# Down projections in rows, in groups of 1024 columns, with seven block products for eight in a third of the k-tile pairs, and weights in 8 KB pieces

## The chip, the cores and the metric

The kernel runs on one core of a Trainium2 chip. A core has a matrix engine (TensorE, PE in the profile), a vector engine (VectorE, DVE), a scalar engine (ScalarE, ACT), a general one (GpSimd, POOL) and a sequencer that issues the DMA transfers here (SyncE, SP). They run side by side, each in the order of its own queue, and wait for one another by semaphores. The metric is the device time of one execution in microseconds; lower is better.

## The reference

Two layers act on a residual stream x of 256 tokens by 2048 features, all in float32. Cut to what matters:

```
for l in range(2):
    h = rms_norm(x, attn_norm[l])
    # w_in: 2048 x 6728; three kinds of heads, 16 in all, and a lightning index
    mixed = concat(moba(h @ w_in), diff(h @ w_in), dsa(h @ w_in))
    x = x + mixed @ w_out[l]                        # 2048 x 2048
    h = rms_norm(x, cross_norm[l])
    x = x + cross_attention(h, mem) @ cross_wo[l]   # 4 heads, 256 memory tokens
    h = rms_norm(x, ffn_norm[l])
    u = h @ ffn_w_up[l]                             # 2048 x 11008
    uc = causal convolution of u over 3 tokens, plus bias
    g, val = split(uc)                              # 5504 features each
    x = x + (silu(g) * val) @ ffn_w_down[l]         # 5504 x 2048
```

The last line of the loop is what the change rewrites: 256 tokens, 5504 inner features (43 k-tiles of 128), 2048 columns.

## The kernel before

TensorE multiplies rounded numbers, so each factor is split in two: a rounded part ("hi") and the rest ("lo", raw minus hi). A product is acts_hi · W_hi + acts_lo · W_hi + acts_hi · W_lo, the product of the two rests being left out. For the weights `load_split` does this: SP issues the load of a piece into the buffer `raw` (L181), ACT rounds it into `hi` (L184) and DVE subtracts, raw − hi, into `lo` (L186). A piece is 4 KB on each partition (2 k-tiles by 512 columns or 4 by 256); there are five buffers for raw and four each for hi and lo. Acts are split by `split`: L163 on ACT, L169 on DVE.

Two helpers hold the matmuls. `mm_rows` has tokens on the output's partitions: for each k-tile and each of two token tiles three matmuls 512 columns wide (L207, L208, L209). `up_acc` has features on the output's partitions: for each k-tile and each of two feature tiles one matmul 512 wide (L231, the weights' rounded part against the 256 hi and 256 lo acts side by side) and one 256 wide (L232, the weights' rest).

The residual stream lives transposed, features on partitions, in `xT`. `residual` adds a projection to it: for each of 8 pairs of feature tiles it runs `up_acc`, copies the second half out of PSUM (L284, ACT), adds (L287, L288, DVE), multiplies by the next norm's gain and splits (L163, L169) and sums squares (L296 on ACT, L297 on POOL).

The down projection of layer 0 is such a `residual` call: 8 pairs of outputs, 43 k-tiles each. That of layer 1 goes by rows: four calls of `mm_rows` on 512 columns, whose results are added (L941) to the stream's rows, which 32 transposes on TensorE (L930) have brought back meanwhile, and stored (L942). The acts of the down projection are split once, in `gate`, at the end of the up stage. That stage is `up_acc` with a convolution behind it (L887 to L895).

The order of the work comes from a tile framework: pools hand out buffers by tag, a piece's write waits until the buffer's last reader is done, and every engine's queue follows the order in which the program was written, moved a little by the framework. `kp` is a pool of 53 slots of 2 KB a partition, for rows, transposed acts and heads. Attention, norms and transposes stand in generators ("flows"); `tick` (L141), called after each weight piece, lets those that are due take a step.

Of the kernel before, what the change touches and what calls it, by code (L numbers as in the profile page):

```python
# [32 lines left out]
FIRST_COL = 3328  # L33

# [6 lines left out]
def hybrid_trunk(ctx: ExitStack, tc: tile.TileContext, x, mem, positions, attn_norm, w_in,  # L41
# [7 lines left out]
    kp = ctx.enter_context(tc.tile_pool(name="kp", bufs=53))  # L49
# [5 lines left out]
    def slot(dt=F32):  # L55
        return kp.tile([P, CH], dt, tag="k", name="k")
# [10 lines left out]
    # ---------------------------------------------------------------- residual stream and constants  # L67
# [6 lines left out]
    for c in range(NCH):  # L74
        xrow.append([slot() for _ in range(NT)])
        for t in range(NT):
            nc.sync.dma_start(xrow[c][t], x[0, t * P:(t + 1) * P, c * CH:(c + 1) * CH])
        raw = wp.tile([P, 2, CH], F32, tag="raw", name="raw", bufs=5)
        nc.sync.dma_start(raw, wfirst[:, 2 * c:2 * c + 2, FIRST_COL:FIRST_COL + CH])
        first_raw.append(raw)  # L80
# [79 lines left out]
    def split(*parts):  # L160
        """parts: (dst, src, gain or None); dst [P, 512] = rounded part | rest of src * gain, src [P, 256]."""
# [12 lines left out]
    def load_split(runs, a, n, raw=None):  # L174
        """weights [P, a, n] from DRAM, by runs of columns -> rounded part and rest."""
        if raw is None:
            raw = wp.tile([P, a, n], F32, tag="raw", name="raw", bufs=5)
# [5 lines left out]
        hi = wp.tile([P, a, n], F32R, tag="hi", name="hi")  # L183
        nc.scalar.activation(hi, raw, AF.Copy)  # L184
        lo = wp.tile([P, a, n], F32R, tag="lo", name="lo")
        nc.vector.tensor_tensor(lo, raw, hi.bitcast(F32), OP.subtract)  # L186
        return hi, lo

    def mm_rows(acts, wview, cols, order, raws=(), ahead=None):
        """[tokens, n] = acts^T w[:, cols]; cols: runs (first, width) of columns; order: pairs (or  # L190
        single ones) of k-tiles that are neighbours in w. -> one PSUM tile for each token tile."""
# [3 lines left out]
        for gi, grp in enumerate(order):  # L195
# [15 lines left out]
            tick(ins)  # L211
        return outs

    def up_acc(wview, runs, acts, order=None, whole=False):
        """two tiles of features on the partitions: w^T acts, the products of the rests of acts
        (with the weights' rounded parts) in the second half, or, if whole, added to the others."""
        outs = [pmm() for _ in range(2)]
        order = order or QUADS
        first = True
        for gi, grp in enumerate(order):  # L220
# [14 lines left out]
            tick(ins)  # L235
        return outs

    QUADS = [tuple(range(k, k + 4)) for k in range(0, KT, 4)]
    PAIRS = [(k, k + 1) for k in range(0, KT, 2)]
# [29 lines left out]

    def residual(acts, wview, order, g, tiles, rest=None, whole=False):  # L270
        """the stream takes in w^T acts; its k-tiles times their gain -> tiles; rx["r"]: the tokens'
        factors, rest is called after them."""
        acc = tp.tile([P, CH], F32, tag="acc", name="acc", bufs=1)
        for i in range(KT // 2):
            outs = up_acc(wview, [(2 * i * P, 2 * P)], acts, order, whole)
# [13 lines left out]
            for k in (2 * i, 2 * i + 1):  # L289
                tiles[k] = slot(F32R)  # L290
            split(*[(tiles[k], xT[:, k, :], g[:, k:k + 1]) for k in (2 * i, 2 * i + 1)])
            if i == 0:
                nc.scalar.activation(acc, pair, AF.Square)
            else:
                sq = tmp()
                nc.scalar.activation(sq, pair, AF.Square)  # L296
                nc.gpsimd.tensor_tensor(acc, acc, sq, OP.add)  # L297

        def factors():
            yield G_R  # L300
            pt = pat()
            for t in range(NT):
                for j in range(2):
                    nc.tensor.matmul(pt[:, t:t + 1], lhsT=acc[:, j * S + t * P:j * S + (t + 1) * P],
                                     rhs=ones[:, 0:1], start=(j == 0), stop=(j == 1))
            a = sp.tile([P, NT], F32, tag="rms_a", name="rms_a")
            nc.vector.tensor_scalar(a, pt[:, :NT], 1.0 / D, EPS, op0=OP.mult, op1=OP.add)
            rx["r"] = rsqrt(a, NT, "rx")
            if rest is not None:
                yield 1  # L310
                rest()

        step(factors())

    # ---------------------------------------------------------------- rotary angles
# [71 lines left out]
    def lambdas():  # L387
        """scalars of the differential attention: -lambda of each layer"""
# [112 lines left out]
    def new_ri():  # L501
        return sp.tile([P, 2, NT], F32, tag="ri", name="ri")
# [23 lines left out]
    def diff_pair(qTs, kTs, scs, vs, nlam, gain, mixT, base):  # L526
# [34 lines left out]
        for i in range(2):  # L561
            mixT[base + i] = slot(F32R)
# [410 lines left out]
```

## Time and profile before

| what | value |
| --- | --- |
| median of 3 runs | 2541.7 us (2540.06 to 2553.94) |
| span of the profiled execution | 2535.3 us; no time of its own is listed, so 6.4 us lie between the span and the median |
| TensorE, matmuls / weight loads | busy 2519.5 us (99%) / 2171.2 us (86%) |
| VectorE | busy 1784.1 us (70%) |
| ScalarE | busy 1385.8 us (55%) |
| GpSimd | busy 158.7 us (6%) |
| down stage of layer 0 | 1035.2 to 1273.7 us |
| down stage of layer 1 | 2293.3 to 2531 us |

The profile's times are of one execution, and the times of the stages are counted from the start of the span. A row such as `L186 DVE TENSOR_TENSOR lo<-raw,hi 128x1024 ... x81 | 99.3, 1225 | 111.9 <-ACT hi L184` is a group of 81 instructions of line 186 on VectorE: 99.3 us busy, 1225 ns for one on the mean, 111.9 us of idle time in front of them, ended mostly by line 184 on ScalarE. In the timeline a row begins with the start and the time busy. A row of windows gives the stretch, its length, and the busy time and instruction count of each engine in it, in the order of its heading.

### The profile page before, as it was taken

The numbers are of one execution on the slowest core, as the hardware profiler recorded it, in microseconds if no ns is written. First come the engines' busy times: TensorE is split into PE (matmuls) and PEld (weight loads), VectorE is DVE, ScalarE is ACT, GpSimd is POOL, SyncE is SP. The second block draws the span as 40 slices with busy tenths as digits, with TensorE's granted clock in tenths as the row PEclk, the third lists the DMA queues.
The fourth block names the chain that finished last, engine by engine and source line by source line (L and its number), as shares of the span: only waits on it lengthen the run. The fifth ranks groups of instructions, "written<-read, shape, count | busy, mean of one in ns | idle before, by whom it ended". The sixth has DMA issues, their size and how long they took to land.

```text
span 2535.3 us, 37663 instructions
## 1 busy us (share of the span) xinstructions
PE 2519.5 (99%) x13798; PEld 2171.2 (86%) x13798; DVE 1784.1 (70%) x3178; ACT 1385.8 (55%) x2148; POOL 158.7 (6%) x177
## 2 busy tenths in 40 slices
PE   8999999999999999999999999999999999999999
PEld 7778888898888888888897788888988888888887
DVE  7876877677777777655568767766777777775444
ACT  6555566566555555544445555655655555555333
POOL 2110211010000000000011011010100000000000
PEclk9999999999999999999999999999999999999999
DMA  7545556556666666666664555565566666665664
GB/s 241 159 146 171 164 174 192 183 159 186 191 191 190 188 189 191 188 193 188 192 171 146 170 167 167 182 191 158 176 189 189 190 191 191 191 190 178 199 202 145
DMA packets 425503, 460.11 MB, mean 181 GB/s; under 512 B 17967, under 2 KB 382437, under 8 KB 425317
## 3 DMA queue, kind: packets, MB, share of 16 engines
q1 hardware_dynamic: 425316, 457.70, 59.9%
q8 instruction: 108, 1.77, 0.3%
q14 instruction: 79, 0.64, 0.1%
HBM read 455.54 MB, written 2.10 MB: 181 GB/s over the span
## 4 chain that ended last, share of the span: by engine, by line
PE 96%; DVE 2%; DMA 1%; issue 1%; ACT 0%; SPq 0%; POOL 0%; DVEq 0%; POOLq 0%
PE mm L231 36%; PE mm L232 19%; PE mm L207 12%; PE mm L208 11%; PE mm L209 11%; PE at L477 1%; DVE lo L186 1%; PE at L452 1%; DMA k<-in_ffn_conv_b_dram 1%; PE at L580 1%; PE at L521 0%; PE at L247 0%; DVE k L169 0%; PE at L816 0%; PE at L851 0%
## 5 line engine op out<-in xcount | busy, mean ns | idle before, releaser
L186 DVE TENSOR_TENSOR lo<-raw,hi 128x1024 fp32r<-128x1024 f32 (+2 forms) x904 | 1061.4, 1176 | 549.9 <-ACT hi L184 528.9
L231 PE MATMUL mm<-k,hi 128*128 128x512 f32 x4080 | 1420.8, 392 | 0.0
L184 ACT ACTIVATE hi<-raw 128x1024 fp32r<-128x1024 f32 (+2 forms) x904 | 912.2, 1012 | 853.0 <-PE mm L231 422.9
L232 PE MATMUL mm<-k,lo 128*128 128x256 f32 x4208 | 1179.3, 280 | 1.5 <-DVE lo L186 1.5
L231 PEld LDWEIGHTS mm<-k,hi 128*128 128x128 f32 x4080 | 763.6, 187 | 168.9
L232 PEld LDWEIGHTS mm<-k,lo 128*128 128x128 f32 x4208 | 795.6, 189 | 2.8 <-DVE lo L186 2.5
L207 PE MATMUL mm<-hi,k 128*128 128x512 f32 (+2 forms) x1432 | 549.9, 384 | 0.0
L208 PE MATMUL mm<-hi,k 128*128 128x512 f32 (+2 forms) x1432 | 534.0, 373 | 0.0
L209 PE MATMUL mm<-lo,k 128*128 128x512 f32 (+2 forms) x1432 | 533.2, 373 | 0.7 <-DVE lo L186 0.7
L207 PEld LDWEIGHTS mm<-hi,k 128*128 128x128 f32 x1432 | 269.8, 188 | 49.8 <-ACT hi L184 2.9
L209 PEld LDWEIGHTS mm<-lo,k 128*128 128x128 f32 x1432 | 269.2, 188 | 49.4 <-issue 1.3
L208 PEld LDWEIGHTS mm<-hi,k 128*128 128x128 f32 x1432 | 270.0, 189 | 44.4 <-issue 2.0
L887 ACT ACTIVATE t<-mm 128x256 f32<-128x256 f32 x172 | 65.4, 380 | 131.0 <-PE mm L232 131.0
L297 POOL TENSOR_TENSOR acc<-acc,t 128x512 f32<-128x512 f32 x35 | 50.4, 1440 | 1115.0 <-ACT t L296 1115.0
L890 DVE TENSOR_TENSOR t<-mm,t 128x256 f32<-128x256 f32 x172 | 72.4, 421 | 53.5 <-ACT t L887 53.4
L892 ACT ACTIVATE t<-t,cw 128x256 f32<-128x256 f32 x172 | 102.6, 598 | 5.5 <-DVE t L891 2.2
L895 DVE SCALAR_TENSOR_TENSOR t<-t,cw 128x254 f32<-128x254 f32 x172 | 81.9, 477 | 1.6
L893 DVE SCALAR_TENSOR_TENSOR t<-t,cw 128x255 f32<-128x255 f32 x172 | 82.1, 478 | 0.0
L891 DVE TENSOR_TENSOR t<-t,R 128x256 f32<-128x256 f32 x172 | 72.3, 422 | 2.9
L486 ACT ACTIVATE k<-t,nb,sc 128x128 f32<-128x128 f32 x80 | 43.1, 540 | 56.4 <-DVE nb L483 56.4
L423 POOL TENSOR_TENSOR t<-k,tab 128x256 f32<-128x256 f32 x32 | 29.0, 906 | 457.6 <-ACT k L433 372.7
L169 DVE SCALAR_TENSOR_TENSOR k<-xT,gains,k 128x256 fp32r<-128x256 f32 x80 | 43.3, 583 | 0.6 <-ACT k L163 0.6
(199 smaller groups left out, 1385.5 us busy)
## 6 DMA issues: line engine op xcount, KB each, us to landing
raw<-in_ffn_w_up_dram SPq DMA_DIRECT2D x336, 512.0 KB, 3.7
raw<-in_ffn_w_down_dram SPq DMA_DIRECT2D x164, 512.0 KB, 3.8
raw<-in_w_in_dram SPq DMA_DIRECT2D x288, 256.0 KB, 3.1
raw<-in_w_in_dram SPq DMA_DIRECT2D x48, 512.0 KB, 3.6
raw<-in_w_out_dram SPq DMA_DIRECT2D x48, 512.0 KB, 3.4
raw<-in_cross_wkv_dram SPq DMA_DIRECT2D x32, 512.0 KB, 3.8
raw<-in_w_in_dram SPq DMA_DIRECT2D x32, 292.0 KB, 3.0
raw<-in_w_out_dram SPq DMA_DIRECT2D x32, 256.0 KB, 3.4
```

The costliest lines, as they stand in the source:

```text
L184: nc.scalar.activation(hi, raw, AF.Copy)
L186: nc.vector.tensor_tensor(lo, raw, hi.bitcast(F32), OP.subtract)
L207: nc.tensor.matmul(o, lhsT=xh, rhs=hi[:, j, :], start=first, stop=False)
L208: nc.tensor.matmul(o, lhsT=xl, rhs=hi[:, j, :], start=False, stop=False)
L209: ins = nc.tensor.matmul(o, lhsT=xh, rhs=lo[:, j, :], start=False, stop=last)
L231: nc.tensor.matmul(outs[i], lhsT=wh, rhs=acts[k], start=first, stop=False)
L232: ins = nc.tensor.matmul(outs[i][:, :S], lhsT=wl, rhs=acts[k][:, :S], start=False, stop=last)
L890: nc.vector.tensor_tensor(u, outs[i][:, :S], v, OP.add)
L891: nc.vector.tensor_tensor(u, u, R, OP.mult)
L892: nc.scalar.activation(v, u, AF.Identity, scale=cw[:, 2, f:f + 1], bias=cw[:, 3, f:f + 1])
L893: nc.vector.scalar_tensor_tensor(v[:, 1:], u[:, :S - 1], cw[:, 1, f:f + 1], v[:, 1:], op0=OP.mult, op1=OP.add)
L895: nc.vector.scalar_tensor_tensor(v[:, 2:], u[:, :S - 2], cw[:, 0, f:f + 1], v[:, 2:], op0=OP.mult, op1=OP.add)
```

## The change

Both layers' down projections now go by rows, in two groups of 1024 columns (`GW`), in a new function `down`. Its unit is a pair of k-tiles: 2 token tiles by 2 k-tiles of acts, times 2 k-tiles by 2 halves of 512 columns of weights. Written as 2 by 2 blocks that is eight block products, three matmuls each. In 7 of the 21 pairs (`SEVEN`: 2, 5, 8, 11, 14, 16, 18) seven products of sums of blocks take their place, of which three are of weights as they are and four of sums of weights. The sums are made on VectorE: of acts (four blocks of 128, L298 to L301, three instructions) and of weights (four blocks of 512, L303 to L305, into one buffer `sum`); both kinds are split like any other, so that such a pair has four splits instead of two. The 43rd k-tile stands alone, at place 10 of group 0's order and place 1 of group 1's. Eight PSUM banks hold a group's results, four for plain products and products 2, 3, 4 (8, 4, 3, 2 in the pool `mm`) and four for the others (1, 5, 6, 7 in `at`). `combine` puts them together (L335 on ACT, L336, L337, L332 on DVE).

Layer 0 then turns each group's rows back, by 16 transposes (L1075), adds them to `xT` (L1078) and runs `take`, the second half of the old `residual`. Layer 1 fetches each group's rows by `back` ahead of the group, and stores from `combine`. `gate` no longer splits the acts; `parts` (L264 to L268) does so in the down stage, in each group anew.

Elsewhere: weights come in pieces of 8 KB a partition (4 k-tiles by 512 columns, 8 by 256), with three buffers each for raw, hi and lo; the first projection of layer 0 keeps its pairs. `tick` still comes every 2 k-tiles by rows and every 4 else. The pool of slots falls from 53 to 38, with 8 half slots (tag `a`) that also hold the odd heads' outputs; rope tables, the sums of squares and the spread token factors move into slots.

```
+KP, AP, RAWS, HIS = 38, 8, 3, 3
+SEVEN = frozenset((2, 5, 8, 11, 14, 16, 18))
+GW = 2 * CH
...
-    kp = ctx.enter_context(tc.tile_pool(name="kp", bufs=53))
+    kp = ctx.enter_context(tc.tile_pool(name="kp", bufs=KP))
...
+    def halves(src, a, n):
+
+        hi = wp.tile([P, a, n], F32R, tag="hi", name="hi", bufs=HIS)
+        nc.scalar.activation(hi, src, AF.Copy)
+        lo = wp.tile([P, a, n], F32R, tag="lo", name="lo", bufs=HIS)
+        nc.vector.tensor_tensor(lo, src, hi.bitcast(F32), OP.subtract)
+        return hi, lo
...
+    PLAIN = {(1, 1): 8, (1, 0): 4, (0, 1): 3, (0, 0): 2}
+
+    def parts(src, n):
+        h, lo = half_slot(), half_slot()
+        nc.scalar.activation(h[:, :n], src[:, :n], AF.Copy)
+        nc.vector.tensor_tensor(lo[:, :n], src[:, :n], h[:, :n].bitcast(F32), OP.subtract)
+        return h, lo
+
+    def down(act, wview, col, order):
...
+            nc.tensor.matmul(bank[q], lhsT=x[0], rhs=w[0], start=first, stop=False)
+            nc.tensor.matmul(bank[q], lhsT=x[1], rhs=w[0], start=False, stop=False)
+            return nc.tensor.matmul(bank[q], lhsT=x[0], rhs=w[1], start=False, stop=left[q] == 0)
...
+            if i in SEVEN:
+                b = new_raw(4, CH)
+                nc.sync.dma_start(b[:, 0, :], wview[:, k, col + CH:col + GW])
+                nc.sync.dma_start(b[:, 1, :], wview[:, k, col:col + CH])
+                last_load[0] = nc.sync.dma_start(b[:, 2:4, :].rearrange("p n c -> p (n c)"),
+                                                 wview[:, k + 1, col:col + GW])
+                s = tmp()
+                a4, s4 = (v.rearrange("p (b t) -> p b t", t=P) for v in (act[i], s))
+                nc.vector.tensor_tensor(s4[:, 0:2, :], a4[:, 0::3, :], a4[:, 1:2, :].to_broadcast([P, 2, P]),
+                                        OP.subtract)
+                nc.vector.tensor_tensor(s4[:, 2, :], s4[:, 1, :], a4[:, 0, :], OP.add)
+                nc.vector.tensor_tensor(s4[:, 3, :], a4[:, 2, :], s4[:, 2, :], OP.subtract)
+                tt = wp.tile([P, 4, CH], F32, tag="sum", name="sum", bufs=1)
+                nc.vector.tensor_tensor(tt[:, 0:2, :], b[:, 1::2, :], b[:, 0:1, :].to_broadcast([P, 2, CH]), OP.add)
+                nc.vector.tensor_tensor(tt[:, 2, :], tt[:, 1, :], b[:, 1, :], OP.add)
+                nc.vector.tensor_tensor(tt[:, 3, :], tt[:, 2, :], b[:, 2, :], OP.add)
+                a = parts(act[i], 4 * P)
+                w = halves(b[:, 1:4, :], 3, CH)
+                sx = parts(s, 4 * P)
+                wt = halves(tt, 4, CH)
...
+                for q in (1, 2, 3, 5, 7, 6, 4):
+                    ins = product(q, *todo[q])
+            else:
+                b = new_raw(m, GW)
+                last_load[0] = nc.sync.dma_start(b, wview[:, k:k + m, col:col + GW])
+                a = parts(act[i], m * S)
+                w = halves(b, m, GW)
...
+    def combine(bank, res, fresh, done=lambda c: None):
...
+        nc.scalar.activation(q1, bank[1], AF.Copy)
+        nc.vector.tensor_tensor(m, bank[6], q1, OP.subtract)
+        nc.vector.tensor_tensor(n, m, bank[7], OP.subtract)
...
         def gate(f, g, v):
+            if f % 2 == 0:
+                act[f // 2] = slot()
             nc.scalar.activation(g, g, AF.Silu)
-            nc.vector.tensor_tensor(v, v, g, OP.mult)
-            act[f] = slot(F32R)
-            split((act[f], v, None))
+            nc.vector.tensor_tensor(act[f // 2][:, f % 2 * S:(f % 2 + 1) * S], v, g, OP.mult)
...
-            residual(act, dn, [range(k, min(k + 4, NF)) for k in range(0, NF, 4)], attn_g(l + 1), hT)
-            continue
...
+        for g in range(D // GW):
+            if last:
+                res = back(g)
+            order = list(range(NF // 2))
+            order.insert(1 if g else NF // 4, NF // 2)
+            bank = down(act, dn, g * GW, order)
...
+            combine(bank, res, True)
+            for n in range(2):
+                for h in range(2):
+                    i = 4 * g + 2 * n + h
+                    pt = pat()
+                    for j in range(2):
+                        for t in range(NT):
+                            nc.tensor.transpose(pt[:, j * S + t * P:j * S + (t + 1) * P],
+                                                res[t, n][:, (2 * h + j) * P:(2 * h + j + 1) * P], ident)
+                    pair = xT[:, 2 * i:2 * i + 2, :].rearrange("p k s -> p (k s)")
+                    nc.vector.tensor_tensor(pair, pt, pair, OP.add)
+                    take(i, attn_g(l + 1), hT, acc)
```

What stands in the queues at the places that the prediction speaks of. First VectorE in layer 0's down stage, before, at the change from one pair of outputs to the next (`lo` is a piece's rest, `t` the projection's second half, `xT` the stream, `k` the next norm's acts):

```order
L186 TENSOR_TENSOR lo_11391<-raw_11387,hi_11389 128x1024
L186 TENSOR_TENSOR lo_11413<-raw_11409,hi_11411 128x1024
L287 TENSOR_TENSOR t_11348<-mm_11108,t_11348 128x256
L186 TENSOR_TENSOR lo_11435<-raw_11431,hi_11433 128x1024
L287 TENSOR_TENSOR t_11348<-mm_11109,t_11348 128x256
L288 TENSOR_TENSOR xT_73<-xT_73,t_11348 128x512
L186 TENSOR_TENSOR lo_11457<-raw_11453,hi_11455 128x1024
L169 SCALAR_TENSOR_TENSOR k_11354<-xT_73,gains0_124,k_11354 128x256
```

VectorE in the same stage after the change, in the middle of group 0 at a seven-product pair (`raw_10069`) among plain ones (`a` is the rest of acts, `sum` the sums of weights):

```order
L303 TENSOR_TENSOR sum_10077<-raw_10069 128x1024
L304 TENSOR_TENSOR sum_10077<-sum_10077,raw_10069 128x512
L305 TENSOR_TENSOR sum_10077<-sum_10077,raw_10069 128x512
L81 TENSOR_TENSOR lo_10043<-raw_10035,hi_10041 128x2048
L267 TENSOR_TENSOR a_10082<-k_8561,a_10081 128x512
L81 TENSOR_TENSOR lo_10087<-raw_10069,hi_10085 128x1536
L267 TENSOR_TENSOR a_10090<-t_10073,a_10089 128x512
L81 TENSOR_TENSOR lo_10095<-sum_10077,hi_10093 128x2048
```

The sums now stand ahead of the rest of the plain piece before them (`lo_10043`), and the pair's own two rests follow with the acts' splits between them.

TensorE in layer 0's down stage before, at the first matmuls of a further pair of outputs:

```order
L231 MATMUL mm_11363<-k_6118,hi_11367 128x512
L232 MATMUL mm_11363<-k_6118,lo_11369 128x256
L231 MATMUL mm_11364<-k_6118,hi_11367 128x512
L232 MATMUL mm_11364<-k_6118,lo_11369 128x256
```

TensorE after the change, where group 0 ends (`mm_9451` is its last bank) and group 1 begins (`mm_10352`, `mm_10359`; `k_10269`, `k_10271` are rows that `combine` has written):

```order
L284 MATMUL mm_9451<-hi_10241,a_10238 128x512
L285 MATMUL mm_9451<-lo_10243,a_10237 128x512
L283 MATMUL mm_10352<-hi_10348,a_10344 128x512
L284 MATMUL mm_10352<-hi_10348,a_10345 128x512
L285 MATMUL mm_10352<-lo_10350,a_10344 128x512
L283 MATMUL mm_10352<-hi_10348,a_10344 128x512
L284 MATMUL mm_10352<-hi_10348,a_10345 128x512
L285 MATMUL mm_10352<-lo_10350,a_10344 128x512
L283 MATMUL mm_10359<-hi_10348,a_10344 128x512
L1075 MATMUL at_10284<-ident_106,k_10269 128x128
L1075 MATMUL at_10284<-ident_106,k_10271 128x128
```

Seven matmuls of the next group now stand between the last product and the 16 transposes that read the combined rows.

Third, SP at the start. Before, the fourth load of weights (`raw_99`) follows the rows of x directly:

```order
L77 DMA k_96<-in_x_dram 128x512
L79 DMA raw_99<-in_w_in_dram 128x2x512
L82 DMA k_75<-in_cross_norm_dram 32x128
```

After, with three load buffers, it stands behind eleven small loads, of which these are the last two:

```order
L514 DMA gbm_138<-in_moba_qk_gain_dram 128x512
L518 DMA k_140<-in_diff_lambda_dram 128x512
L96 DMA raw_99<-in_w_in_dram 128x2x512
```

More of the change, by code (lines that the diff above doesn't have):

```diff
@@ L182, in load_split @@
                 o += m
[L183 to L187, printed above, removed]
+        return halves(raw, a, n)
     def mm_rows(acts, wview, cols, order, raws=(), ahead=None):
@@ L238, in hybrid_trunk, with back @@
+    def back(g):
+        res = {}
+        for n in range(2):
+            for t in range(NT):
+                pt = pat()
+                for j in range(4):
+                    nc.tensor.transpose(pt[:, j * P:(j + 1) * P], xT[:, 8 * g + 4 * n + j, t * P:(t + 1) * P], ident)
+                res[t, n] = slot()
+                nc.scalar.activation(res[t, n], pt, AF.Copy)
+        return res
     QUADS = [tuple(range(k, k + 4)) for k in range(0, KT, 4)]
+    EIGHTS = [tuple(range(k, k + 8)) for k in range(0, KT, 8)]
@@ L288, in residual @@
                 nc.vector.tensor_tensor(pair, pair, u, OP.add)
[L289 to L313, printed above, removed]
+            take(i, g, tiles, acc)
+        step(factors(acc, rest))
     HD2 = 64
@@ L402, in rope_table @@
         gb = head_gain[kind][:, l]
-        tb = tp.tile([P, 2, NT, 2, w], F32, tag="tab" + kind, name="tab", bufs=1)
+        tb = [slot()[:, :NT * 2 * w].rearrange("p (t a d) -> p t a d", t=NT, a=2) for _ in range(2)]
         for a in range(2):
@@ L499, in p_T, with mix_slot @@
         return o
+    def mix_slot(h):
+        return half_slot() if h % 2 else slot(F32R)
     def new_ri():
@@ L945 @@
+        if not last:
+            step(factors(acc))
 _INS = ['x', 'mem', 'positions', 'attn_norm', 'w_in', 'moba_qk_gain', 'diff_qk_gain', 'diff_lambda', 'diff_subln',
```

161 lines of the change are left out of this document (111 added, 50 removed).

## The prediction

> **What bounds the kernel.** I read the page first: shares, slices and the chain.
>
> ```profile
> span 2535.3 us, 37663 instructions
> PE 2519.5 (99%) x13798; PEld 2171.2 (86%) x13798; DVE 1784.1 (70%) x3178; ACT 1385.8 (55%) x2148; POOL 158.7 (6%) x177
> DVE  7876877677777777655568767766777777775444
> PEclk9999999999999999999999999999999999999999
> PE 96%; DVE 2%; DMA 1%; issue 1%; ACT 0%; SPq 0%; POOL 0%; DVEq 0%; POOLq 0%
> ```
>
> TensorE is busy 99% of the span and is 96% of the chain, at a granted clock of nine tenths or more in every slice: only fewer or shorter matmuls can gain, and any work that another engine cannot hide loses. DVE is at 70%, so cover exists, but not everywhere: I then asked for windows of the up stage (560 to 1015) and of the two down stages, the third and the first row.
>
> ```profile
> core 0: us, PE busy (x) PEld busy (x) DVE busy (x) ACT busy (x) POOL busy (x), PEclk, DMA share, GB/s
> 1035.00:1273.00 238.00, 238.00 (x1375) 209.83 (x1374) 128.37 (x134) 106.94 (x129) 8.66 (x6) 1.00 0.61 189
> 2293.00:2531.00 238.00, 238.00 (x1067) 196.86 (x1065) 109.81 (x103) 94.54 (x99) 0.00 (x0) 1.00 0.58 183
> 560.00:1015.00 455.00, 454.48 (x2626) 400.45 (x2625) 356.11 (x582) 264.52 (x405) 0.73 (x1) 1.00 0.66 192
> ```
>
> Each down stage is one closed block of matmuls, with DVE busy 128 and 110 of 238 us. The timeline dates its ends:
>
> ```profile
> 1035.23 0.39 PE L231 MATMUL mm<-k,hi 128*128 128x512 f32 x1
> 1273.73 0.39 PE L207 MATMUL mm<-hi,k 128*128 128x512 f32 x1
> 2293.26 0.39 PE L207 MATMUL mm<-hi,k 128*128 128x512 f32 x1
> 2298.75 0.60 PE L930 MATMUL at<-ident,xT 128*128 128x128 f32 x4
> 2299.10 0.48 PE L207 MATMUL mm<-hi,k 128*128 128x512 f32 x1
> 2530.95 0.39 PE L209 MATMUL mm<-lo,k 128*128 128x512 f32 x1
> ```
>
> **Matmuls.** Layer 0's down stage is 1273.73 − 1035.23 = 238.5 us, for 8 × 43 × 2 pairs of a 512-wide and a 256-wide matmul. Layer 1's is 2530.95 − 2293.26 + 0.2 (the last one) = 237.9 us for 4 × 43 × 6 = 1032 matmuls 512 wide and 32 transposes. Four transposes push the next matmul from 2298.75 to 2299.10, 0.35 us, so 32 take 2.8. One matmul is (237.9 − 2.8)/1032 = 0.2278 us from start to start; busy time of one (0.39) overlaps its neighbours and is no price.
>
> After the change a layer has two groups, each of 7 pairs by 21 matmuls, 14 by 24 and the single k-tile by 12: 495, so 990 for 1032. Layer 1 loses 42 × 0.2278 = 9.6 us. Layer 0 gets the row form, 990 × 0.2278 = 225.5, and 32 transposes, 2.8, in place of 238.5: 10.2 less. Together −19.8.
>
> **VectorE in the down stage.** Prices of operations there and nearby:
>
> ```profile
> L186 DVE TENSOR_TENSOR lo<-raw,hi 128x1024 fp32r<-128x1024 f32 x81 | 99.3, 1225 | 111.9 <-ACT hi L184 111.7
> L186 DVE TENSOR_TENSOR lo<-raw,hi 128x512 fp32r<-128x512 f32 x4 | 2.8, 694 | 4.3 <-ACT hi L184 4.3
> L184 ACT ACTIVATE hi<-raw 128x1024 fp32r<-128x1024 f32 x81 | 85.9, 1061 | 128.0 <-PE mm L208 126.2 <-issue 1.7
> L184 ACT ACTIVATE hi<-raw 128x512 fp32r<-128x512 f32 x4 | 2.5, 632 | 6.6 <-PE mm L208 6.6
> L890 DVE TENSOR_TENSOR t<-mm,t 128x256 f32<-128x256 f32 x172 | 72.4, 421 | 53.5 <-ACT t L887 53.4
> L941 DVE TENSOR_TENSOR k<-mm,k 128x512 f32<-128x512 f32 x7 | 4.8, 689 | 11.6 <-PE mm L209 11.6
> L169 DVE SCALAR_TENSOR_TENSOR k<-xT,gains,k 128x256 fp32r<-128x256 f32 x80 | 43.3, 583 | 0.6 <-ACT k L163 0.6
> L297 POOL TENSOR_TENSOR acc<-acc,t 128x512 f32<-128x512 f32 x35 | 50.4, 1440 | 1115.0 <-ACT t L296 1115.0
> ```
>
> The subtraction grows by (1225 − 694)/512 = 1.037 ns an element, so 2048 take 2.29 us and 1536 1.76 (estimates along that line), 128 take 0.29; on ACT 1.92 and 1.49.
>
> - A plain pair is 5.47 us of TensorE (24 × 0.2278); VectorE does one subtraction of weights 2048 wide (2.29) and one of acts (0.69): 2.98.
> - A seven-pair is 4.78 us of TensorE. VectorE does three sums of acts (0.42 + 0.29 + 0.29), three of weights (1.23 + 0.69 + 0.69), two splits of acts (1.38) and two of weights (1.76 + 2.29): 9.04.
>
> So a seven-pair borrows 4.3 us from what plain pairs leave, 2.5 each. A group is 7 × 9.04 + 14 × 2.98 + 1.65 = 106.7 us, its combination 10 or 12 operations at 0.65 (6.5 in layer 0, 7.8 in layer 1), and in layer 0 the return to the stream some 7.6 (four adds at 0.69, eight splits at 0.58, which the 1440 ns squares on POOL may stretch). Against 495 × 0.2278 + 1.4 = 114.2 of TensorE that is 120.8 in layer 0, 114.5 in layer 1. Whether it fits hangs on how closely VectorE packs:
>
> ```profile
> 1016.99 1.23 DVE L186 TENSOR_TENSOR lo<-raw,hi 128x1024 fp32r<-128x1024 f32 x1
> 1018.13 0.48 DVE L893 SCALAR_TENSOR_TENSOR t<-t,cw 128x255 f32<-128x255 f32 x1
> 1018.67 1.06 ACT L184 ACTIVATE hi<-raw 128x1024 fp32r<-128x1024 f32 x1 [0.91 <-PE mm L231]
> 1019.76 1.23 DVE L186 TENSOR_TENSOR lo<-raw,hi 128x1024 fp32r<-128x1024 f32 x1 [0.64 <-ACT hi L184]
> ```
>
> Behind a subtraction of 1.23 an independent operation starts after 1.14: 0.09 less. Some 70 neighbours in a group are independent, so 106.7 becomes 100.3, and the totals 114.4 in layer 0 and 108 in layer 1: just covered, or level. [...]
>
> **Where covering fails.** From rounding to its subtraction the hand-over is immediate (1018.67 + 1.06 to 1019.76). But rounding waits for TensorE to free a buffer, 363 times and 1.2 us on the mean behind L231:
>
> ```profile
> engine line waited for: us in total, times, longest us
> ACT hi L184 <- PE mm L231: 422.9, 363, 2.4
> DVE lo L186 <- ACT hi L184: 528.9, 459, 3.0
> ```
>
> With three buffers of 8 KB a piece's rounding starts when TensorE ends the piece three earlier. I walked this by hand over P, P, S (two plain, one seven). VectorE's 15.0 (14.1 packed) stands against 15.7 of TensorE, and the next rest is ready 4.2 to 4.4 us behind the end that released it, where 5.2 are at hand: 0.8 to 1 us spare, no wait. Where S and P alternate (pairs 14 to 18) it is 11.3 against 10.2, a loss of 1.1 twice that the lead of the pieces before pays. Stalls remain where that lead is zero: about 1.3 at the start of each layer's down stage (one plain piece must be rounded, subtracted and its acts split, none of it before the acts exist), 2.6; at the change of groups, where the combination's 6.5 to 7.8 us stand in the queue ahead of the next rests and the PSUM banks come free one by one, 2.0 in layer 0 and 1.0 in layer 1; at the entry to layer 1, whose k-tiles 8 to 15 come 7 to 17 us after the last product while tiles 0 to 7 give TensorE 48 × 0.2278 = 10.9 of work, 0.5. Bounds for the 6.1 together: 0 where the lead holds, 14 where each costs a whole combination (twice 6.5).
>
> **Edits taken at nothing.** Splitting acts in the down stage twice rather than once at the gate: counted above; the up stage, where DVE has 99 us free, gets lighter to no use. Weights in 8 KB pieces elsewhere: the same elements in fewer instructions, under a TensorE that is 96% of the chain. The fourth load at the start:
>
> ```profile
> 8.43 0.38 SPq L79 DMA_DIRECT2D raw<-in_w_in_dram  x1
> 16.88 0.43 SPq L384 DMA_DIRECT2D k<-in_diff_lambda_dram  x1
> 22.91 1.22 DVE L186 TENSOR_TENSOR lo<-raw,hi 128x1024 fp32r<-128x1024 f32 x1
> raw<-in_w_in_dram SPq DMA_DIRECT2D x288, 256.0 KB, 3.1
> raw<-in_ffn_w_down_dram SPq DMA_DIRECT2D x164, 512.0 KB, 3.8
> ```
>
> With three load buffers it moves on SP behind eleven small loads, issued at about 17 and, at 3.8 us, there at 21; its subtraction is at 22.91 anyway: 0, at most 2. The tail keeps its shape (two last adds and their stores): 0 ± 1. The seven-pair's three loads land on one tile: 0.7 us from 3.1 at 256 KB to 3.8 at 512 KB puts 1 MB at some 5.2, and buffer, load, sums and subtraction come round in 16.5 against 15.7 in group 0: taken as hidden, since the second plain pair has slack; if not, 0.8 × 14 = 11.
>
> **Sum.** −9.6 − 10.2 + 6.1 = −13.7, against an execution whose span is 2535.3 with 6.4 us around it to the median 2541.7, which I keep: 2528.0, 0.54% less. Half a per cent (12.7 us) is about what a measurement of this kernel can tell from no change, so the bounds are 2529.0 and 2554.4.
>
> **Rivals.**
> - Everything is hidden: stalls of 0 to 2, hence 2519 to 2524. For it: the stages' DVE shares of 128 and 110 in 238; against it: the combination has no cover but the lead.
> - VectorE never overlaps, so that a group in layer 0 takes 120.8 where TensorE takes 114.2. Then 2541.7 − 19.8 + 13.2 + 3.6 (the starts, and layer 1's change) = 2539. Against it: the 0.09 above. [...]
> - The 1 MB loads come round too late: 2533 to 2545, by the 11 above.
> - The rest of the kernel suffers from 38 slots for 53: in the attention's projections an evacuation on ACT waits for a slot that a head still uses, and behind it in ACT's queue the rounding of the next weights. TensorE holds two more chunks of outputs in PSUM, but only three rounded pieces, 16 us. At 0 to 15 us a layer: 2530 to 2558. For it: heads' work is spread over the whole stage; against it: eight half slots take in half of the attention's outputs, and TensorE reaches the releasing matmul before.
> - On the other side, VectorE becomes the bound of both down stages: if three buffers let the lead reach over one pair only, a seven-pair is 4.26 short and gets back 2.49 from one plain pair; 1.77 × 28 = 50, so 2572. It passes the bound of slower from 1.16 us a seven-pair (32.5 us). For it: the 363 waits show that rounding has no lead beyond its buffers; against it: the walk, with 0.8 us spare.
>
> **Chances.** Forecast (2523.5 to 2534) 0.42; all hidden 0.15; no overlap 0.10; late loads 0.08; slots 0.10; VectorE the bound (2545 to 2575) 0.15. Six tenths of the forecast lies below 2529.0: faster 0.41. Beyond 2554.4 lie most of the last case and some of the slots': slower 0.20. Same 0.39. The range from 2520 to 2556 leaves out some 0.04 below and 0.13 above.
>
> **What would show it.** Right: the down stages take about 229 to 232 us each, DVE some 220 busy in them, matmuls 990 a layer with start to start 0.228; idle TensorE stands only at a stage's start and at the change of groups. Wrong: waits of products for sums' rests at every seven-pair (VectorE the bound); waits of a subtraction for its load (late loads); idle TensorE before 450 us or between 1600 and 1750 (slots); a matmul price other than 0.228 in the row form of layer 0.

## The result, and the profile after

The changed kernel takes 2556.0 us (median of 20 runs, 2549.6 to 2567.8) where the kernel before, in runs beside it, takes 2542.0; the ratio over all runs is 1.0043 with a 95% interval of 1.0027 to 1.006. So it is a little slower. Forecast were 2528.0 us and a gain of 0.54%; the time stands at the very upper edge of the range from 2520 to 2556, and the change went the other way.

The page after, the lines that answer to those shown of before:

```profile
span 2554.4 us, 34687 instructions
PE 2514.4 (98%) x13402; PEld 2146.4 (84%) x13402; DVE 1910.2 (75%) x2982; ACT 1364.4 (53%) x1756; POOL 162.8 (6%) x177
DVE  6876766677777777889968767666777777778888
PEclk9999999999999999999999999999999999999999
```

TensorE has 396 matmul instructions fewer and still the span is 19.1 us longer. It is no longer busy all of the down stages, which the windows show (the up stage, then the two down stages):

```profile
core 0: us, PE busy (x) PEld busy (x) DVE busy (x) ACT busy (x) POOL busy (x), PEclk, DMA share, GB/s
558.00:1039.00 481.00, 478.92 (x2769) 422.04 (x2768) 355.37 (x495) 247.72 (x307) 3.84 (x3) 1.00 0.61 191
1039.00:1277.00 238.00, 230.06 (x1010) 188.42 (x1009) 216.63 (x233) 138.97 (x133) 3.98 (x3) 0.99 0.55 190
2310.00:2551.00 241.00, 230.90 (x1008) 187.68 (x1006) 207.69 (x223) 131.49 (x124) 0.00 (x0) 0.99 0.52 177
```

Who waits for whom in these two stages: of TensorE in layer 0 and layer 1, then of VectorE in layer 0 and layer 1 (total us, times, longest):

```profile
PE mm L285 <- DVE lo L81: 7.7, 6, 3.5
...
PE mm L285 <- DVE lo L81: 8.0, 8, 2.5
...
DVE sum L303 <- DMA raw<-in_ffn_w_down_dram: 10.3, 7, 2.3
DVE lo L81 <- ACT hi L79: 9.0, 9, 2.5
...
DVE sum L303 <- DMA raw<-in_ffn_w_down_dram: 14.9, 8, 2.7
DVE lo L81 <- ACT hi L79: 11.4, 8, 2.5
```

TensorE waits for rests of weights, and VectorE, which makes them, waits 25.2 us for loads at its sums of weights. The timeline shows one such case (VectorE, ScalarE, the queue of loads and the matmul that waited):

```profile
1095.51 1.75 DVE L81 TENSOR_TENSOR lo<-raw,hi 128x1536 fp32r<-128x1536 f32 x1
...
1097.29 0.34 SPq L292 DMA_DIRECT2D raw<-in_ffn_w_down_dram  x1
...
1098.14 0.43 SPq L294 DMA_DIRECT2D raw<-in_ffn_w_down_dram  x1
1099.98 0.68 DVE L267 TENSOR_TENSOR a<-k,a 128x512 fp32r<-128x512 f32 x1
1100.51 1.92 ACT L79 ACTIVATE hi<-raw 128x2048 fp32r<-128x2048 f32 x1 [2.37 <-issue]
...
1102.98 1.23 DVE L303 TENSOR_TENSOR sum<-raw 128x1024 f32<-128x1024 f32 x1 [2.31 <-DMA raw<-in_ffn_w_down_dram]
1104.24 0.69 DVE L304 TENSOR_TENSOR sum<-sum,raw 128x512 f32<-128x512 f32 x1
...
1104.85 2.28 DVE L81 TENSOR_TENSOR lo<-raw,hi 128x2048 fp32r<-128x2048 f32 x1
...
1107.19 0.50 PE L285 MATMUL mm<-lo,a 128*128 128x512 f32 x1 [1.32 <-DVE lo L81]
```

The load of a seven-product pair is issued at 1097.29, the moment that the subtraction on the piece three places ahead of it ends (1095.51 + 1.75) and frees its buffer. VectorE reaches that pair's first sum at 1100.67 and stands there until 1102.98, when the load has landed. Behind the first two of these sums in its queue stands the rest of a plain piece (the first of the two between this pair and the seven-product pair before), whose rounded part is ready at 1102.43. It starts only at 1104.85, and TensorE, free from 1105.87 on, waits for it until 1107.19. Started at 1102.43 it would have ended at 1104.71, before TensorE was free.

To see where the time went, each profiled execution is cut by its timeline: a down stage runs from its first matmul to the first of the next stage (or to the last matmul's end). "Outside" is the rest of the span.

| kernel | down, layer 0 | down, layer 1 | outside | up stages at 353 ns |
| --- | --- | --- | --- | --- |
| before | 238.5 | 238.1 | 2058.7 | 0 |
| the change | 237.6 | 240.6 | 2076.2 | 0 |
| e1_no_seven | 237.1 | 236.0 | 2094.8 | 2 |
| e2_half_ops | 234.2 | 239.2 | 2078.7 | 1 |
| e3_sums_late | 229.4 | 228.6 | 2096.2 | 2 |
| e4_raw4 | 229.3 | 226.5 | 2085.9 | 1 |
| e5_raw4_half | 229.0 | 226.5 | 2070.3 | 0 |
| e6_raw4_nine | 236.0 | 229.6 | 2088.6 | 1 |
| e7_all | 229.5 | 226.9 | 2071.6 | 0 |
| e8_slots | 237.2 | 240.0 | 2077.8 | 0 |
| e9_cross_small | 229.8 | 226.4 | 2087.9 | 2 |
| e10_order_only | 229.5 | 228.4 | 2092.8 | 1 |

The last column counts up stages whose pairs of matmuls came 353 ns apart instead of 346, which costs about 9 us a stage; it seems to change from run to run of the same kernel and is told of at the end. Each kernel has one profiled execution, so this is read from the times: those of e9_cross_small stand in three groups near 2528, 2536 and 2546 us, and its profiled execution, with two such stages, is of the last. Those of the kernel before spread from 2537 to 2565 us. The two kernels' profiles compared above have none, so their difference is not of this kind: 19.1 us, of which 1.6 in the down stages and 17.5 outside.

### The profile page after: what moved, and what is told of

Read it like the earlier page. It is cut to its first block, busy times and chain, and to the rows that moved or that the text cites. A ratio compares the mean times of both kernels' runs of the same rounds, so it can differ in the third digit from the quotient of the medians.

```text
span 2554.4 us, 34687 instructions
## 1 busy us (share of the span) xinstructions
PE 2514.4 (98%) x13402; PEld 2146.4 (84%) x13402; DVE 1910.2 (75%) x2982; ACT 1364.4 (53%) x1756; POOL 162.8 (6%) x177
## 5 line engine op out<-in xcount | busy, mean ns | idle before, releaser
L81 DVE TENSOR_TENSOR lo<-raw,hi 128x2048 fp32r<-128x2048 f32 (+4 forms) x466 | 969.7, 2084 | 356.0 <-ACT hi L79 354.7
L245 PE MATMUL mm<-k,hi 128*128 128x512 f32 x3136 | 1098.4, 393 | 3.2 <-DVE xT L437 3.2
L79 ACT ACTIVATE hi<-raw 128x2048 fp32r<-128x2048 f32 (+4 forms) x466 | 811.2, 1744 | 434.5 <-PE mm L221 164.0
L246 PE MATMUL mm<-k,lo 128*128 128x256 f32 x3264 | 914.4, 280 | 0.1
L245 PEld LDWEIGHTS mm<-k,hi 128*128 128x128 f32 x3136 | 586.8, 187 | 133.2 <-issue 3.5
L246 PEld LDWEIGHTS mm<-k,lo 128*128 128x128 f32 x3264 | 617.1, 189 | 0.8 <-DVE lo L81 0.5
L220 PE MATMUL mm<-hi,k 128*128 128x512 f32 (+2 forms) x1088 | 413.8, 380 | 0.0
L221 PE MATMUL mm<-hi,k 128*128 128x512 f32 (+2 forms) x1088 | 404.3, 372 | 0.0
L285 PE MATMUL mm<-lo,a 128*128 128x512 f32 x548 | 216.4, 395 | 15.7 <-DVE lo L81 15.7
L283 PE MATMUL mm<-hi,a 128*128 128x512 f32 x548 | 214.6, 392 | 0.2 <-DVE t L1027 0.2
L284 PE MATMUL mm<-hi,a 128*128 128x512 f32 x548 | 214.4, 391 | 0.0
L1040 ACT ACTIVATE t<-t 128x256 f32<-128x256 f32 x86 | 35.7, 418 | 229.3 <-DVE t L1032 229.3
L283 PEld LDWEIGHTS mm<-hi,a 128*128 128x128 f32 x548 | 103.7, 189 | 21.6 <-issue 0.6
L284 PEld LDWEIGHTS mm<-hi,a 128*128 128x128 f32 x548 | 103.6, 189 | 21.8
```

The source lines that it names most:

```text
L79: nc.scalar.activation(hi, src, AF.Copy)
L81: nc.vector.tensor_tensor(lo, src, hi.bitcast(F32), OP.subtract)
L220: nc.tensor.matmul(o, lhsT=xh, rhs=hi[:, j, :], start=first, stop=False)
L221: nc.tensor.matmul(o, lhsT=xl, rhs=hi[:, j, :], start=False, stop=False)
L245: nc.tensor.matmul(outs[i], lhsT=wh, rhs=acts[k], start=first, stop=False)
L246: ins = nc.tensor.matmul(outs[i][:, :S], lhsT=wl, rhs=acts[k][:, :S], start=False, stop=last)
```

## The experiments

All ratios are to the kernel before, with their 95% intervals.

**No seven-product pairs.** `combine` then only adds the four banks.

```
-SEVEN = frozenset((2, 5, 8, 11, 14, 16, 18))
+SEVEN = frozenset()
```

> Part left alone: the form by rows in groups of 1024, the 8 KB pieces and the 38 slots; taken out: all seven-product pairs (every pair by eight products, 1032 matmuls a layer, and a combination of four operations a group). Theory (the seven-product pairs lose by waits for rests and sums what they save in matmuls): matmuls cost 84 x 0.2278 = 19.1 us more, the waits in the down stages fall from some 24 us to 3 to 6, so the kernel stays at the time of the change within 5 us, about 2556 us, and each down stage is 239 to 242 us. Rival (the waits belong to the groups and the large loads, not to the seven-product pairs): they stay, and the kernel is 15 us or more slower than the change, 2570 us or above.

Measured: 2569.0 us, ratio 1.007 (1.0044 to 1.0097). By the total, 13 us above the change, the rival seems to win, but both up stages of its profile ran at 353 ns; the down stages themselves are not longer than the theory had them (239 to 242 us) but shorter:

```profile
1050.00:1286.00 236.00, 235.07 (x1044) 194.24 (x1044) 137.36 (x111) 109.07 (x100) 4.01 (x3) 1.00 0.57 191
2328.00:2563.00 235.00, 235.00 (x1047) 194.84 (x1046) 124.87 (x96) 103.03 (x94) 0.00 (x0) 1.00 0.55 178
```

TensorE is busy 235 of 235 us in layer 1 and 235.07 of 236 in layer 0: all but some 0.9 us of the waits in the down stages go with the seven-product pairs (and with the longer combination that they bring). With them the stages are 237.6 and 240.6 us long, without them 237.1 and 236.0.

**Long instructions outside the down stages.**

```
-        nc.scalar.activation(hi, src, AF.Copy)
...
+        step = a // 2 if fine and a * n > 2 * CH and a % 2 == 0 else a
+        for j in range(0, a, step):
+            nc.scalar.activation(hi[:, j:j + step, :], src[:, j:j + step, :], AF.Copy)
+        for j in range(0, a, step):
+            nc.vector.tensor_tensor(lo[:, j:j + step, :], src[:, j:j + step, :],
+                                    hi[:, j:j + step, :].bitcast(F32), OP.subtract)
...
-        return halves(raw, a, n)
+        return halves(raw, a, n, True)
```

> As the change, but outside the down stages every 8 KB piece is rounded and subtracted in two instructions of 1024 elements instead of one of 2048; loads and buffers stay. Theory (outside the down stages the change loses some 17 us because a rounding or subtraction twice as long stands in front of the short chains that TensorE waits for: squares, factors, stream adds): 8 to 14 us faster than the change, the stages from the output projection to the up stage back within 2 us of before. Rival (the loss there is from 38 slots for 53, or from three buffers): within 3 us of the change.

Measured: 2552.1 us, ratio 1.0018 (0.9991 to 1.0046), not clearly apart from before or from the change. Its part outside is 2078.7 with one up stage at 353 ns, so some 2070 without: 6 us less than the change, below what the theory asked for and above its rival. What it mends is seen behind layer 0's output projection. In the change, from the stream's add on:

```profile
456.75 1.92 ACT L79 ACTIVATE hi<-raw 128x2048 fp32r<-128x2048 f32 x1 [3.11 <-PE mm L221]
...
458.57 0.89 ACT L180 ACTIVATE k<-xT,gains 128x256 fp32r<-128x256 f32 x2
...
459.37 0.62 ACT L407 ACTIVATE t<-xT 128x512 f32<-128x512 f32 x1
...
460.12 1.98 POOL L408 TENSOR_TENSOR k<-k,t 128x512 f32<-128x512 f32 x1 [12.72 <-ACT t L407]
...
462.16 1.05 PE L416 MATMUL at<-ones,k 128*128 128x1 f32 x8 [1.37 <-POOL k L408]
```

and in this experiment:

```profile
457.02 1.29 POOL L412 TENSOR_TENSOR k<-k,t 128x512 f32<-128x512 f32 x1 [10.78 <-ACT t L411]
...
459.07 0.95 PE L420 MATMUL at<-ones,k 128*128 128x1 f32 x8
```

The matmuls that sum the squares stand in TensorE's queue, and TensorE stops for them. In the change a rounding of 1.92 us stands ahead of the squares on ScalarE; with rounding in halves the squares come 3 us sooner and TensorE does not wait.

**Sums behind the rest of the piece before.**

```
+                with tc.issue_after(last_lo[0].ins):
+                    nc.vector.tensor_tensor(tt[:, 0:2, :], b[:, 1::2, :], b[:, 0:1, :].to_broadcast([P, 2, CH]), OP.add)
...
```

> As the change, but the three sums of weights of a seven-product pair are held in VectorE's queue until behind the rest of the piece before (same work, another order). Theory (a sum that waits for its load blocks the rest of the plain piece queued behind it, 10.3 us in layer 0's down stage): the waits of products in the down stages fall from some 22 us to 8 to 12, the kernel is 10 to 14 us faster than the change. Rival (VectorE lacks time at the seven-product pairs whatever the order): within 3 us of the change, the waits moving from the plain piece to the sums' own rests; or slower.

Measured: 2555.5 us, ratio 1.0015 (0.9993 to 1.0037): by the total, the rival. But both up stages of its profile ran at 353 ns, and the stages that it changes are 8.2 and 12.0 us shorter than in the change:

```profile
1048.00:1277.00 229.00, 226.96 (x1006) 186.63 (x1005) 212.36 (x231) 138.36 (x132) 4.00 (x3) 1.00 0.58 196
2322.00:2551.00 229.00, 226.61 (x1005) 186.65 (x1003) 206.15 (x222) 131.48 (x123) 0.00 (x0) 1.00 0.54 184
```

Its fastest run, 2538.5 us, lies 17.5 below the profiled one, which is what two such stages cost. The order of VectorE's queue, with no work less, takes 20 us out of the two down stages. Its sums, asked for later, now wait for loads 0.4 and 3.3 us in the two layers, where it was 10.3 and 14.9.

**A fourth load buffer**, paid for by slots and temporary tiles.

```
-KP, AP, RAWS, HIS = 38, 8, 3, 3
+KP, AP, RAWS, HIS = 36, 8, 4, 3
...
-        return tp.tile([P, CH], F32, tag="t", name="t", bufs=8)
+        return tp.tile([P, CH], F32, tag="t", name="t", bufs=6)
```

> As the change, but four load buffers of 8 KB for three, paid for by 36 slots for 38 and 6 temporary tiles for 8. Theory (the seven-product pair's load is issued only when the third buffer comes free, and lands after VectorE asks for it): the 10.3 us that VectorE waits for loads in layer 0's down stage shrink to under 2, and the down stages take 228 to 233 us each instead of 238 and 241; the rest of the kernel loses 0 to 6 us by fewer slots; 8 to 18 us faster than the change in all. Rival (VectorE lacks time at the seven-product pairs): the waits for loads vanish but products wait for rests as long as before, within 4 us of the change.

Measured: 2534.1 us, ratio 0.9951 (0.9934 to 0.9968): faster than before, and some 22 us below the change. The two down stages:

```profile
1049.00:1278.00 229.00, 226.95 (x1007) 186.93 (x1006) 214.61 (x230) 138.72 (x132) 4.00 (x3) 1.00 0.56 196
2312.00:2537.00 225.00, 225.00 (x1002) 186.53 (x1001) 205.98 (x221) 130.88 (x122) 0.00 (x0) 1.00 0.53 183
```

What VectorE still waits for in layer 0's:

```profile
DVE lo L81 <- ACT hi L79: 12.0, 8, 2.2
DVE sum L303 <- DMA raw<-in_ffn_w_down_dram: 1.2, 1, 1.2
```

The waits for loads fall from 10.3 to 1.2 us, and in layer 1 TensorE is busy throughout, as in the first experiment, with 42 matmuls fewer and 236.0 − 226.5 = 9.5 us less.

**The price of the fourth buffer alone.**

```
-KP, AP, RAWS, HIS = 38, 8, 3, 3
+KP, AP, RAWS, HIS = 36, 8, 3, 3
...
-        return tp.tile([P, CH], F32, tag="t", name="t", bufs=8)
+        return tp.tile([P, CH], F32, tag="t", name="t", bufs=6)
```

> A control: the change with three load buffers and only the price that was paid for the fourth, 36 slots for 38 and 6 temporary tiles for 8. Theory (slots and temporary tiles play no part): the time of the change within 4 us, the down stages at 236 to 242 us each and the attention stages as in the change. Rival (fewer temporary tiles hold VectorE back and so changed the down stages): down stages under 233 us; or rival (slots are short): the attention stages longer by 3 us or more.

Measured: 2558.9 us, ratio 1.0044 (1.0017 to 1.0071), the change again; down stages of 237.2 and 240.0 us. So the two slots and two temporary tiles given up did not make the gain. No run gave back the 15 slots that the change takes away; that they did not make the loss outside is read from layer 0's attention alone. From its first matmul to the output projection, layer 0's attention part takes 344.1 us before, 343.1 in the change, 345.3 here and 342.9 with four load buffers, with 53, 38, 36 and 36 slots.

**Both remedies, and the order on top.** The fourth buffer with the rounding in halves; and then the sums behind the rest of the piece before as well.

> Four load buffers (36 slots, 6 temporary tiles) and, outside the down stages, two instructions of 1024 for one of 2048. Theory (late loads and long instructions ahead of short chains are two separate losses that add): the down stages as with four load buffers alone (226 to 230 us each) and the rest 6 to 9 us shorter, so 2522 to 2528 us where the up stages run at 345 ns a pair of matmuls. Rival (one of the two only moves the other's wait): no faster than four load buffers alone, 2532 to 2534 us.

> As e5_raw4_half, and the sums of weights held behind the rest of the piece before. Theory (with loads in time the order no longer matters): within 2 us of e5_raw4_half. Rival (order and loads are separate losses): some 3 us faster, layer 0's down stage at 226 to 227 us.

Measured: 2536.6 us, ratio 0.9948 (0.9925 to 0.9971), its fastest run 2527.6; and 2533.0 us, ratio 0.994 (0.9913 to 0.9966), its fastest 2528.6. By the medians neither is clearly faster than the fourth buffer alone. But in both profiles all up stages ran at 346 ns, with spans of 2525.8 and 2528.0, and outside the down stages the fourth buffer with halves takes 2070.3 us, against 2076.2 in the change and some 2077 with the fourth buffer alone (2085.9 less one stage at 353 ns). Read by stages, then, the two remedies add, and with loads in time the order is worth nothing. These two, the fourth buffer alone and e9_cross_small below beat both kernels; the four intervals overlap.

**Nine seven-product pairs**, with four load buffers.

```
-SEVEN = frozenset((2, 5, 8, 11, 14, 16, 18))
+SEVEN = frozenset((2, 4, 6, 8, 10, 12, 14, 16, 18))
```

> Four load buffers (36 slots, 6 temporary tiles) and nine seven-product pairs a group (2, 4, 6, 8, 10, 12, 14, 16, 18) instead of seven. By the price list two more pairs save 12 matmuls a layer, 2.7 us, and add 12.1 us to VectorE in each group, which then has some 112 us packed beside 113 of TensorE before combination and return. Theory (VectorE was just covered with seven): it becomes the bound, the down stages take 234 to 242 us each instead of 229 and 226. Rival (VectorE has room): 223 to 227 us each.

Measured: 2545.4 us, ratio 1.0002 (0.9981 to 1.0023); down stages of 236.0 and 229.6 us.

```profile
1049.00:1285.00 236.00, 228.74 (x995) 183.56 (x994) 232.10 (x262) 145.41 (x140) 4.00 (x3) 1.00 0.57 190
2321.00:2550.00 229.00, 225.99 (x992) 183.45 (x990) 224.81 (x254) 138.50 (x130) 0.00 (x0) 1.00 0.53 179
```

VectorE is busy 98% of both: it is the bound in layer 0 (6.7 us slower than with seven) and about level with TensorE in layer 1 (3.1 us slower), where the forecast of 234 at least was too high.

**Small pieces in the cross-attention's output projection**, and the order without the buffer.

```
-        residual(coT, cwo, [[range(2), range(2, 4)]] + [[range(4)]] * 7, gB[:, (2 * L + l) * KT:(2 * L + l + 1) * KT], h3, spread, whole=True)
+        residual(coT, cwo, [[range(2), range(2, 4)]] * 8, gB[:, (2 * L + l) * KT:(2 * L + l + 1) * KT], h3, spread, whole=True)
```

> As e5_raw4_half (four load buffers, two instructions of 1024 outside the down stages), and the cross-attention's output projection in pieces of 2 k-tiles by 256 columns as before, instead of 4. Theory (what is left of the loss at the entry to each up stage, three waits of 0.7 us a layer against 1.1 us before, comes from these pieces): 2 to 4 us faster than e5_raw4_half, 2523 to 2526 us where the up stages run at 346.6 ns a pair. Rival (it comes from the multiplications by gains, which take 1.9 us for two beside the sums on GpSimd whatever the piece): within 1 us of e5_raw4_half.

> Three load buffers, 38 slots and 8 temporary tiles as in the change; the sums of weights held behind the rest of the piece before, two instructions of 1024 outside the down stages and the small pieces of e9_cross_small. Theory (the order of VectorE's queue alone takes the harm out of a late load): down stages of 228 to 230 us each, within 4 us of e9_cross_small. Rival (loads still late show once the rest is faster): down stages above 233 us and 8 us or more behind e9_cross_small.

Measured: 2536.2 us, ratio 0.9965 (0.9942 to 0.9987), and 2550.6 us, ratio 1.0023 (1.0004 to 1.0042). For the first the rival held: with both up stages at 353 ns its part outside is 2087.9, some 2070 without, as in e5_raw4_half. For the second the theory held in its stages (229.5 and 228.4) and missed the total: less the stages at 353 ns, its part outside is some 14 us longer than that of e9_cross_small. With small pieces in three buffers TensorE waits 6.1 and 5.7 us in the two layers between the cross attention's values and the end of the up stage, where it waits 3.4 and 3.3 in e9_cross_small, and in the same stretches its granted clock is at half for 13.6 us, against 3.4.

## Why the prediction was wrong

The forecast for the span was 2535.3 − 13.7 = 2521.6 us; the profiled execution has 2554.4, 32.8 more. With the 2.8 us of transposes that now lie outside them, the down stages take 481.0 us where 462.9 were forecast, 18.1 more; the other 14.7 lie outside.

- **Matmuls: right.** 42 fewer in a layer were to save 9.6 us in layer 1; with nothing else in the way (e4_raw4 against e1_no_seven) they saved 9.5.
- **VectorE's time: right.** Seven pairs a group were just covered once loads came in time, nine were not; of some 220 us forecast VectorE was busy 216.6 and 207.7. (The combination in layer 0 has 8 operations on VectorE, not the 10 of the sum, and the four adds and eight splits of the return make 7.4 us, not 7.6: 1.5 us too much a group, which changes nothing here.) The rival in which VectorE becomes the bound did not happen: it lacked its work's data, not time. Its operations do start before the one before them ends, here by 0.08 us (the next row ends at 1095.59, and the row that begins the change's timeline starts at 1095.51), so the rival without overlap fell too.

```profile
1094.90 0.69 DVE L305 TENSOR_TENSOR sum<-sum,raw 128x512 f32<-128x512 f32 x1
```

- **The load of 1 MB: the step that failed.** I put its round at 16.5 us against 15.7 and took it as hidden, "since the second plain pair has slack". The size was a little too small. The first row below is of plain pieces, the second of the last of a seven-product pair's three loads:

```profile
raw<-in_ffn_w_down_dram SPq DMA_DIRECT2D x56, 1024.0 KB, 5.6
raw<-in_ffn_w_down_dram SPq DMA_DIRECT2D x32, 512.0 KB, 5.2
```

  In the case shown above all three took 5.7 us from the first issue to the landing (1097.29 to 1102.98), where 5.2 were put, and the sums then waited 1.7 us on the mean (25.2 in 15 times), where 0.8 was the forecast for the bad case. But the larger error is what was left out, what stands behind the sum that waits: the queue printed with the change has the sums ahead of the plain piece's rest, so a late load of one pair stops the products of another. Added up over the starts of matmuls in the timeline, TensorE lost 22.3 us in waits of over 0.1 us in the two down stages and 2.4 at half speed behind the longest of them, where 5.6 were forecast there. The longest wait (3.5 us, until 1168.82) is at the change of groups, where the return of the rows to the stream stands in VectorE's queue too, behind a sum that waited 1.9 us for its load; 2.0 were forecast for that place. The late-load rival had the late load, with 11 us for twice that, and a chance of 0.08.
- **8 KB pieces elsewhere, "taken at nothing": failed.** Outside the down stages the kernel loses 17.5 us, of which 2.8 are transposes that the sum had counted in the down stages. Long roundings and subtractions ahead of short chains are 6 of the rest (e2_half_ops, e5_raw4_half). The cover named, a TensorE that is 96% of the chain, is no cover where TensorE itself stops for such a chain.
- **The entry to layer 1:** 0.5 us forecast. With the remedies its first projections and attention are still 5.2 us longer than before (343.7 for 338.5), of which 1.4 are the 16 transposes; the squares on GpSimd, which now come at once at the end, hold TensorE for 1.6 us, and 1.6 us more than before go to matmuls at half speed.
- **The entries to the up stages**, from the cross attention's output projection on, keep some 3 us each over before with the remedies. Small pieces did not mend them; that the multiplications by gains beside GpSimd's sums do it (two take 1.9 us there in the change and 0.9 before) was only argued, and stays open.
- **Slots:** no sign of the rival. Layer 0's attention is no longer than before, and what layer 1's is longer by goes mostly to the transposes, the squares and the half speed named above; no run with more slots tested it.
- **The base.** 6.4 us were taken to lie around the span; the changed kernel's profiled execution lists 2556.2 for a span of 2554.4, so 1.8. The median of three was of executions a little slower than the profiled one, and the forecast 4.6 us too long by it, which made the miss look smaller.

## What to carry to other kernels

A transfer that came a little late cost little by itself here; it cost what stood behind its first reader in that engine's queue: with the same work in another order (e3_sums_late) VectorE still waited 0.4 and 3.3 us for loads, and the two down stages were 20.2 us shorter. When a step that reads new data is written or scheduled ahead of one that is needed sooner, count its wait on the path of the later one; either move it behind (no memory) or give the load one buffer more, and check on which of the two the stage depends. And when pieces are doubled, look for the short chains that share a queue with them and that the bounding engine waits for (some 6 us of the time outside the down stages here).

## What the runs showed of the hardware

**Half speed after a wait.** Layer 1's down stage in the change, TensorE alone:

```profile
2376.46 0.39 PE L284 MATMUL mm<-hi,a 128*128 128x512 f32 x1
2379.32 0.50 PE L285 MATMUL mm<-lo,a 128*128 128x512 f32 x1 [2.48 <-DVE lo L81]
2379.66 0.40 PE L283 MATMUL mm<-hi,a 128*128 128x512 f32 x1
2379.89 0.47 PE L284 MATMUL mm<-hi,a 128*128 128x512 f32 x1
2380.16 0.63 PE L285 MATMUL mm<-lo,a 128*128 128x512 f32 x1
2380.59 0.63 PE L283 MATMUL mm<-hi,a 128*128 128x512 f32 x1
2381.01 0.63 PE L284 MATMUL mm<-hi,a 128*128 128x512 f32 x1
...
2383.53 0.40 PE L284 MATMUL mm<-hi,a 128*128 128x512 f32 x1
2383.78 0.40 PE L285 MATMUL mm<-lo,a 128*128 128x512 f32 x1
```

After 2.86 us between two starts, matmuls 512 wide come 0.427 us apart from 2380.16 to 2383.15, some 3.4 us in all, and cost 1.4 us more; after 2.30 us (at 2450.74) they do not. The granted clock says the same: over the window from 2380.06 to 2383.47 it is 0.50. The slices of the page are too coarse to show it.

The trace of the change has four such stretches of 3.41 us at a granted clock of 0.50 (from 1168.33, 1291.21, 1731.53 and 2380.06), that of the kernel before has none within its span. At some 8 matmuls each, 0.2 us longer than usual, they are about 6 of the 19.1 us, an estimate that takes in the 2.4 and 1.6 us above: by it these waits cost more than their own length. The gaps that the four belong to are 3.92 (the first begins inside it), 2.59, 1.76 and 2.86 us from start to start, those of 2.59 and 1.76 with eight matmuls one column wide behind them, so the length alone does not tell them from the gap of 2.30 us. The starts of the stretches lie 122.88, 440.32 and 648.53 us apart, 36, 129 and 190 times 3.413. What decides whether a gap is followed by half speed was not shown: this is one trace, and no run tested it by itself.

**Two rhythms of the same matmuls.** The same 400 us of layer 0's and layer 1's up stage, in the change and with four load buffers (the first count is matmuls):

```profile
600.00:1000.00 400.00, 400.00 (x2310) 352.69 (x2309) 290.97 (x402) 204.93 (x254) 0.00 (x0) 1.00 0.60 190
1880.00:2280.00 400.00, 400.00 (x2309) 352.71 (x2308) 290.28 (x400) 204.98 (x254) 0.00 (x0) 1.00 0.60 190
```

```profile
600.00:1000.00 400.00, 400.00 (x2266) 346.81 (x2266) 285.90 (x396) 201.92 (x251) 0.00 (x0) 1.00 0.59 185
1880.00:2280.00 400.00, 400.00 (x2310) 352.69 (x2309) 290.23 (x399) 205.50 (x256) 0.00 (x0) 1.00 0.61 190
```

2310 or 2266 matmuls in the same time, at a granted clock of 1.00 and with TensorE busy throughout: a pair of a 512-wide and a 256-wide matmul takes 346 or 353 ns, and a stage keeps its rhythm to the end, which makes it some 9 us longer or shorter. Both rhythms occur in one execution. What picks one was not found; a difference of 0.4% between two kernels of this sort is read only by stages.
